# A tuned sum of reciprocals: new list for the last 48 rows, three large first loads, interleaved half rows

## Chip, cores, metric

The kernel runs on one core of one Trainium2 chip. The metric is the device time of one execution in microseconds (us), given as the median of several executions. Because this case turns on how executions of one and the same program differ, whole sets of executions are told beside the medians.

## The reference

```python
def setup_inputs():
    batch, seq, dim = 32, 512, 1024
    return {"x": np.abs(np.random.randn(batch, seq, dim)).astype(np.float32) + 1e-6}

def reference(x):
    return np.sum(1.0 / x, axis=-1).astype(np.float32)
```

There are 16,384 sums of 1024 reciprocals. On the chip they lie as 128 partitions by 128 rows. In what follows a "row" is one of these 128 columns of sums: a block of 128 x 1024 floats, 512 KB.

## The kernel before

The kernel takes the reciprocals of a pair of elements a and b from one logarithm and one exponential: 1/a + 1/b = (a + b) · exp(−ln(ab)). Each row is therefore split into two halves of 512, and several engines share the work. A static list gives the order of all operations; each letter is an operation, the number after it a row, `+n` means n rows in one instruction, `@b` a bank of PSUM or a slot of the product tile.

| letter | engine | what it does for a row |
|---|---|---|
| D | SP (load queue) | loads rows into a ring of 40 |
| P | POOL | product of the two halves, 128 x 512 |
| W | DVE | the same product, both halves read from SBUF |
| C, V | PE, DVE | PE copies the second half to PSUM; DVE multiplies the first half by that copy |
| L | ACT | logarithm of the product |
| E | ACT | exponential of minus the logarithm: in place, or to PSUM when it has a bank |
| S | PE | sum of the two halves in PSUM by two matmuls with the identity |
| R | DVE | final multiply and accumulate: 512 wide where the row has an S, else 1024 wide with the exponential broadcast |

The last two rows are handled as four half rows, numbered 126 to 129, so that less work stands behind the last load.

```python
    PLAN = """
        D9 D10 D14 D7 P0+2 C3@3 S2@0 V3 P2 L0+2@0 S3@1 E0+2@6 P4+2 S6@2 L2+2@2 R0 E2+2 R1
        # ... cut ...
        E122 R120 P124 S124@3 L123@8 R122 E123@7 W125 L124@15 S125@0 R123 P126 L125@16 E124
        P127 E125 R124 P128 S128@1 L126@17 R125 L127@0 P129 E126@7 S129@2 E127@6 R126 L128@1
        L129@9 R127 E128 E129 R128 R129
    """.split()
    # ... cut ...
    def place(r):                        # row -> row of the ring, offset, width of a half
        if r < LAST:                     # LAST = 126, F = 128, H = 512
            return r, 0, H
        q, part = divmod(r - LAST, 2)
        return LAST + q, part * H, H // 2
    # ... cut: note() keeps the dependences; its core is the loop that the change touches ...
        for other in needed:
            o_inst, o_engine, o_tick, _, _, o_known = other
            if o_tick <= known.get(o_engine, 0):
                tc.declare_no_dep(inst, o_inst, reason="implied by other waits")
                continue
            if o_engine == engine:
                continue
    # ... cut ...
            elif op in "WV":
                w = place(r)[2]
                in1 = xs(r, 1) if op == "W" else ps[:, copied[r], :w]
                inst = nc.vector.tensor_tensor(
                    out=prod[:, p, :w], in0=xs(r, 0), in1=in1, op=mult
                )
    # ... cut ...
            elif op == "R":
                # row: the exponential's slot (S rows) or the ring's row (the others)
                inst = nc.vector.tensor_tensor_reduce(
                    out=row, in0=row, in1=other, scale=S,
                    scalar=total if q in summed else 0.0,
                    op0=mult, op1=add, accum_out=total,
                )
```

## Time and profile before

| | before |
|---|---|
| time, median | 169.65 us (169.61 to 170.13) |
| span of the profiled run | 167.5 us |
| last load landed | 161.60 us |
| DVE done | 164.97 us |
| PE / DVE / ACT / POOL busy | 79 / 76 / 79 / 78% |
| W products / V products | 3 / 17 |

The prediction below reads the load queue, the landings and the tail. Three more lines of the same page matter later. PEclk is the granted clock of PE in 40 slices of the span, in tenths of full speed (9 is full); the next line is the group of W products (count, then busy us and mean ns of one); the last gives the shares of the chain of work that ended last.

```profile
PEclk9999999999699999999999999999999999999998
...
DMA 64%; DVE 11%; POOL 8%; PE 7%; ACT 5%; issue 2%; SPq 0%; DVEq 0%; POOLq 0%
...
L217 DVE TENSOR_TENSOR prod<-ring 128x512 f32<-128x512 f32 x3 | 2.0, 688 | 0.0
```

The reader is to see that the chain is 64% load time, and that one slice of PEclk, the 11th (42 to 46 us), reads 6. The timeline of PE shows what stands before it: a wait of 5.65 us for a load, in brackets.

```profile
43.64 2.08 PE L206 MATMUL ps<-ring,ident 128*128 128x512 f32 x2 [5.65 <-DMA ring<-in_x_dram]
```

I saw this 6 before predicting and made nothing of it.

### The profile page before, as it was taken

What the parts mean: (1) busy time and instruction counts of PE and PEld (TensorE: products, weight loads), DVE (VectorE), ACT (ScalarE), POOL (GpSimd) and SP (SyncE); (2) the same over time, 40 slices, a digit from 0 to 9 for tenths busy, and PEclk for the clock granted to TensorE, in tenths of its full rate; (3) what the DMA queues carried; (4) which work ended last, traced back from release to release, by engine and by line L of the source; (5) the groups of instructions that cost most, each with busy time, mean ns of one, the idle gap of its engine ahead of it and who ended that gap; (6) DMA issues with size and microseconds to landing.
All of it is one profiled execution on the core that took longest, in us unless ns stands there. A gap on an engine that the chain in (4) does not pass through costs nothing.

```text
span 167.5 us, 1308 instructions
## 1 busy us (share of the span) xinstructions
PE 132.1 (79%) x290; PEld 54.5 (33%) x290; DVE 127.5 (76%) x280; ACT 131.5 (79%) x155; POOL 131.0 (78%) x83
## 2 busy tenths in 40 slices
PE   0004996880599998999998999989979599977990
PEld 0002432330234343333433434334433144432450
DVE  0000585588049899979897898889999999999993
ACT  3000990994089999689989998999999999899991
POOL 1005946992599994998899998997989998999960
PEclk9999999999699999999999999999999999999998
DMA  6999999999899998998999999999999999999910
GB/s 202 440 431 434 401 470 438 438 438 438 383 438 430 483 446 385 434 460 351 470 431 421 438 417 425 432 420 440 407 429 426 410 425 421 417 407 411 393 63 16
DMA packets 4904, 67.25 MB, mean 402 GB/s; under 512 B 545, under 2 KB 673, under 8 KB 2209
## 3 DMA queue, kind: packets, MB, share of 16 engines
q1 hardware_dynamic: 4896, 67.18, 94.8%
q8 instruction: 2, 0.03, 0.1%
q14 instruction: 6, 0.04, 0.1%
HBM read 67.11 MB, written 0.07 MB: 401 GB/s over the span
## 4 chain that ended last, share of the span: by engine, by line
DMA 64%; DVE 11%; POOL 8%; PE 7%; ACT 5%; issue 2%; SPq 0%; DVEq 0%; POOLq 0%
DMA ring<-in_x_dram 64%; POOL prod L196 8%; DVE ring L264 7%; PE ps L229 4%; DVE prod L264 3%; PE ps L206 3%; ACT prod L239 3%; ACT ps L248 2%; ACT prod L248 1%; DVE prod L217 1%; SPq L184 0%; DVE sums L264 0%; DVEq L264 0%; POOLq L196 0%; DVEq L307 0%
## 5 line engine op out<-in xcount | busy, mean ns | idle before, releaser
L196 POOL TENSOR_TENSOR prod<-ring 128x1024 f32<-128x1024 f32 (+2 forms) x77 | 130.3, 1728 | 31.0 <-DMA ring<-in_x_dram 27.1
L229 PE MATMUL ps<-ring,ident 128*128 128x512 f32 (+1 forms) x256 | 116.3, 599 | 4.6 <-DVE sums L264 3.2
L239 ACT ACTIVATE prod<-prod 128x1024 f32<-128x1024 f32 (+3 forms) x77 | 67.8, 900 | 29.6 <-POOL prod L196 22.3
L264 DVE CUSTOM_DVE_ANT_1 ring<-ring,ps 128x1024 f32<-128x1024 f32 (+1 forms) x65 | 76.3, 1209 | 10.3 <-ACT ps L248 10.2
L229 PEld LDWEIGHTS ps<-ring,ident 128*128 128x128 f32 x256 | 48.3, 194 | 71.8 <-issue 51.1
L264 DVE CUSTOM_DVE_ANT_0 prod<-prod,ps 128x512 f32<-128x512 f32 (+1 forms) x63 | 40.6, 678 | 0.3
L206 PE MATMUL ps<-ring,ident 128*128 128x512 f32 x34 | 19.8, 672 | 26.6 <-DMA ring<-in_x_dram 26.5
L248 ACT ACTIVATE ps<-prod 128x1024 f32<-128x1024 f32 (+3 forms) x40 | 34.1, 859 | 1.4 <-DVE sums L264 0.7
L248 ACT ACTIVATE prod<-prod 128x1024 f32<-128x1024 f32 (+3 forms) x37 | 33.8, 924 | 0.7
L217 DVE TENSOR_TENSOR prod<-ring,ps 128x512 f32<-128x512 f32 x17 | 11.6, 684 | 26.5 <-PE ps L206 26.5
L206 PEld LDWEIGHTS ps<-ring,ident 128*128 128x128 f32 x34 | 6.2, 203 | 36.6 <-issue 18.3
L264 DVE DVE_READ_ACCUMULATOR2_ANT sums<- 128x1 f32 x130 | 10.7, 82 | 0.0
L217 DVE TENSOR_TENSOR prod<-ring 128x512 f32<-128x512 f32 x3 | 2.0, 688 | 0.0
L82 ACT ACT_TABLE_LOAD x1 | 1.3, 1283 | 0.7 <-PEq L296 0.7
L264 DVE CUSTOM_DVE_ANT_1 ring<-ring,ps,sums 128x512 f32<-128x512 f32 x1 | 0.7, 746 | 0.2 <-DVE sums L264 0.2
L264 DVE CUSTOM_DVE_ANT_0 prod<-prod,ps,sums 128x256 f32<-128x256 f32 x1 | 0.5, 479 | 0.2 <-DVE sums L264 0.2
masks.py:197 POOL MEMSET ident<- 128x128 f32 x1 | 0.2, 204 | 0.3 <-POOLq L296 0.3
masks.py:199 POOL TENSOR_SCALAR_AFFINE_SELECT ident<-ident 128x128 f32<-128x128 f32 x1 | 0.3, 293 | 0.1
L296 POOL MEMSET const-float32-0.0<- 128x1 f32 x1 | 0.1, 98 | 0.2 <-issue 0.2
L296 POOL MEMSET const-bfloat16-1.0<- 128x1 bf16 x1 | 0.1, 101 | 0.0
L296 POOL MEMSET const-uint8-127<- 128x1 uint8 x1 | 0.1, 101 | 0.0
L296 POOL MEMSET const-float32-1.0<- 128x1 f32 x1 | 0.1, 98 | 0.0
## 6 DMA issues: line engine op xcount, KB each, us to landing
ring<-in_x_dram SPq DMA_DIRECT2D x3, 3584.0 KB, 31.5
ring<-in_x_dram SPq DMA_DIRECT2D x2, 5120.0 KB, 26.2
ring<-in_x_dram SPq DMA_DIRECT2D x1, 7168.0 KB, 42.0
ring<-in_x_dram SPq DMA_DIRECT2D x1, 6144.0 KB, 33.4
ring<-in_x_dram SPq DMA_DIRECT2D x4, 1536.0 KB, 33.7
ring<-in_x_dram SPq DMA_DIRECT2D x6, 1024.0 KB, 28.9
ring<-in_x_dram SPq DMA_DIRECT2D x2, 2560.0 KB, 32.8
ring<-in_x_dram SPq DMA_DIRECT2D x1, 4608.0 KB, 13.8
```

Source lines behind the costliest of these rows:

```text
L82: nc.scalar.add_instruction(mybir.InstLoadActFuncSet(name=nc.get_next_instruction_name(), act_func_set_id=act_sets.index("natural_log_exp_ ...
L196: inst = nc.gpsimd.tensor_tensor(out=prod[:, p : p + m, :w], in0=ring[:, a : a + m, at : at + w], in1=ring[:, a : a + m, at + w : at + 2 * w],
L206: inst = nc.tensor.matmul(ps[:, b, : place(r)[2]], lhsT=ident, rhs=xs(r, 1), start=True, stop=True,)
L217: inst = nc.vector.tensor_tensor(out=prod[:, p, :w], in0=xs(r, 0), in1=in1, op=mult)
L229: inst = nc.tensor.matmul(ps[:, b, : place(r)[2]], lhsT=ident, rhs=xs(r, h), start=h == 0, stop=h == 1,)
L239: inst = nc.scalar.activation(out=pg, in_=pg, func=Ln, scale=S)
L248: inst = nc.scalar.activation(out=rc, in_=pg, func=Exp, scale=-1.0)
L264: inst = nc.vector.tensor_tensor_reduce(out=row, in0=row, in1=other, scale=S, scalar=total if q in summed else 0.0, op0=mult, op1=add, acc ...
L296: nc = _bacc.Bacc("TRN2", target_bir_lowering=False, num_devices=1)
```

## The change

Its intent is to shorten the tail and to balance the engines in the last 48 rows. There are three parts: a new list (three large first loads of 14, 12 and 14 rows instead of 9, 10, 14 and 7; single rows over the last 14; eight W products instead of three, mostly in rows 82 to 95); the four half rows in interleaved order (first half of row 126, first half of 127, second of 126, second of 127), so that a half never adds to the sum just before it; and bookkeeping that keeps dependences within one engine.

```diff
     PLAN = """
-        D9 D10 D14 D7 P0+2 C3@3 S2@0 V3 P2 L0+2@0 S3@1 E0+2@6 P4+2 S6@2 L2+2@2 R0 E2+2 R1
+        D14 D12 D14 P0+2 C3@3 S2@0 V3 P2 L0+2@0 C11@3 S3@1 E0+2@6 P4+2 V11 L2+2@2 R0 S6@2
 ... cut: the rest of the list; of the changed one, three lines from rows 81 to 99 and the end:
+        L81+2@18 P88+2 S86@2 R83 D1 D1 D1 E81+2 R82 S87@4 L88+2@0 W91 W86 D1 E88+2@6 W87 D1
+        D1 D1 W90 L85+2@20 S94@3 P94 R89 L87@17 E85+2 R88 P92 S95@5 L94@8 R86 E87 P93 R85
+        L90+3@2 R87 C97@7 P96 R81 E94 S98@0 V97 L93@9 P98 R94 L96@5 E93@7 S97@1 W95 E90+3@2
 ... cut ...
+        L119@7 S122@2 E121 R120 P123 L122@15 R121 E122 W124 L123@16 R122 L124@12 E123@7 W125
+        S125@0 E124@6 R123 P126 L125@13 P127 L126@14 S127@1 R124 E125 P128 L127@0 S128@2
+        E126@7 P129 R125 E127 S129@3 L128@1 R126 L129@20 E128 R127 E129 R128 R129
@@ place
-        q, part = divmod(r - LAST, 2)
+        part, q = divmod(r - LAST, F - LAST)
@@ note
+            if o_engine == engine:
+                continue
             if o_tick <= known.get(o_engine, 0):
                 tc.declare_no_dep(inst, o_inst, reason="implied by other waits")
-                continue
-            if o_engine == engine:
                 continue
```

## The prediction

> **What bounds the kernel now.** I read the page first (busy shares, slices, queues), then the waits of the load queue, then the landing time of every load, then the chain that ended last and the DVE timeline of the final microseconds. The page:

> ```profile
> span 167.5 us, 1308 instructions
> PE 132.1 (79%) x290; PEld 54.5 (33%) x290; DVE 127.5 (76%) x280; ACT 131.5 (79%) x155; POOL 131.0 (78%) x83
> ...
> DMA  6999999999899998998999999999999999999910
> ...
> q1 hardware_dynamic: 4896, 67.18, 94.8%
> ```

> Four compute engines are busy some 130 us each, the DMA engines 94.8% of the span, from the first slice to the next to last. So the loads are the floor of the body, and compute has some 30 us of idle to spend. What the queue itself waits for:

> ```profile
> SPq L184 <- DVE sums L264: 95.6, 14, 30.6
> SPq L184 <- DMA ring<-in_x_dram: 44.7, 17, 6.1
> ```

> These 140 us look alarming, but they are waits to *issue*: the load of row 112 was issued at 116.8 and landed at 143.8, so the transfers stay queued behind others. Reading the landings in order (middle one of each load's 16 counts) shows no hole: loads of 1, 2, 3, 7 and 14 rows land 1.28, 2.48, 3.69, 8.52 and 16.94 us after the one before. That is 1.205 us a row plus 0.07 us a load. The 16th count trails the middle one by 1.5 us from about 80 us on; it is the one that releases readers. The last load landed at 161.60, the load of row 125 at 159.01. The loads therefore fix about 161.6 of the 167.5 us. Behind stands a tail: DVE ends at 164.97, the output takes 2.5 us more, and the measured time is 2.1 us over the span (169.65 against 167.5). DVE in the tail:

> ```profile
> 159.04 0.69 DVE L217 TENSOR_TENSOR prod<-ring 128x512 f32<-128x512 f32 x1
> 159.65 1.21 DVE L264 CUSTOM_DVE_ANT_1 ring<-ring,ps 128x1024 f32<-128x1024 f32 x1
> ...
> 160.96 0.69 DVE L264 CUSTOM_DVE_ANT_0 prod<-prod,ps 128x512 f32<-128x512 f32 x1
> ...
> 161.71 0.69 DVE L264 CUSTOM_DVE_ANT_0 prod<-prod,ps 128x512 f32<-128x512 f32 x1
> ...
> 162.36 0.69 DVE L264 CUSTOM_DVE_ANT_1 ring<-ring,ps 128x512 f32<-128x512 f32 x1
> ...
> 163.21 0.75 DVE L264 CUSTOM_DVE_ANT_1 ring<-ring,ps,sums 128x512 f32<-128x512 f32 x1 [0.16 <-DVE sums L264]
> ...
> 163.89 0.41 DVE L264 CUSTOM_DVE_ANT_0 prod<-prod,ps 128x256 f32<-128x256 f32 x1
> ...
> 164.49 0.48 DVE L264 CUSTOM_DVE_ANT_0 prod<-prod,ps,sums 128x256 f32<-128x256 f32 x1 [0.18 <-DVE sums L264]
> ```

> The first is the product of row 125, at 159.04: it starts 0.03 us after its row landed, so the tail hangs on that landing. Then come the sums of rows 123, 124, 125 and of the four half rows. From start to start: a 512-wide step costs 0.61, a 1024-wide 1.14, a half row 0.61 or 0.34 by its form; adding to an earlier sum costs 0.07 more. The two half rows with "sums" among their inputs add to what the row just before them left; where an unheld step starts together with the accumulator read before it (163.89), these two start 0.24 and 0.26 us after it (162.97 and 164.23).

> [...] The kernel waits there, and the trace shows its price, the 0.24 and 0.26 us. [...] instructions with several waits may have EventSemaphore instructions put before them; the trace has them at 21 ns on DVE, with about 0.1 us from one to the held start when the queue has run dry. [...]

> **The change part by part.**

> *Loads.* 34 instead of 33, the same bytes: one more times 0.07. First loads 14, 12, 14 instead of 9, 10, 14, 7. The first rows land at 13.8 + 5 x 1.205 + 0.7 = 20.6 us instead of 14.56, so POOL, ACT and DVE start 6 us later. Is that paid at the end? Load queue: row 40 is needed in flight at 52 us and asks for rows 0 to 11 summed; at 1.03 us a row (DVE in the body: two 1.14 and two 0.61 per four rows plus 0.48 idle on ACT) from about 25 us they are done near 38. Margin 14 us; the same count for the later loads never leaves less than 6. No hole arises. POOL: a row pair takes 2.4, so 1.2 a row, less the one in eight that DVE multiplies, against 1.215 a row of landing. It is level with the landings at the next loads (rows 72 to 79 land at 102.0, P78 ends near 110.4), about where it is now. So the late start is absorbed: 0 us on the end.

> *Last 48 rows.* DVE work from row 80 on, by the list: now 22 rows of 0.61, 24 of 1.14, 10 products of 0.61, halves 1.9, 48.9 us; changed 23, 23, 12, halves 1.9, 49.4 us. Row 79 is summed near 113.8 with one product (0.6) done, leaving 48.8, hence an end of work at 162.6 if never stopped, against 163.3 by the same count now. Both are below the landing-driven end, with 2 us of small gaps to absorb. Single rows over the last 14: rows 114 and 116 land 1.28 us sooner, rows 117 on at the same time. 0 at the end.

> *Same-engine waits.* The edit in the bookkeeping keeps dependences within an engine. In the built order, DVE instructions that wait on DVE go from 2 to 21, POOL on POOL from 1 to 14. Nearly all ask for something long past. At up to 0.1 us each that is 2 us on DVE and 1.3 on POOL, mostly before 150 us where there is idle. In the tail I allow 0.1 to 0.3 us in all.

> *The tail.* The product of row 125 starts at its landing, 159.01 + 0.07 = 159.08, plus 0.03. Then the new order: product 0.61, row 123 1.14, row 124 1.14 (it was 0.61), row 125 0.61, then halves 0.61, 0.34 (was 0.68), 0.41, 0.48. Sum 5.34: 164.45 without gaps. Now the same sum is 0.61+1.14+0.61+0.61+0.61+0.68+0.34+0.48 = 5.08, ending at 164.12; measured 164.97, so gaps cost 0.85, of which 0.50 stand before the two accumulating halves and 0.31 before rows 124 and 125 on ACT and on the second wait. Interleaved, each half adds to the half two back, so most of the 0.50 goes; row 124 takes 1.14, so ACT runs ahead. Gaps left: 0.1 to 0.3. End 164.55 to 164.75, against 164.97.

> Do POOL and ACT allow it? The last half lands at 161.67; POOL's four halves pitch 0.69 and end near 162.7 as now (162.61). Counting ACT at its pitches (0.52 a 512-wide, 0.31 a half), the last exponential starts near 163.35 and ends at 163.75; its sum needs it at about 164.0. Yes, by 0.3 us.

> Sum: +0.07 for the load, +0.19 for the tail's work, -0.55 to -0.75 for its gaps: about -0.3 us. 169.65 - 0.35 = 169.3.

> **The rivals.**

> 1. *The late start is not absorbed.* Compute is then the bound and up to 6 us come at the end: 175. For it: the four engines are within 20% of the loads' rate. Against: 37 us of DVE idle, and POOL waits for loads nine times, 27.1 us in all. I give 2%.
> 2. *The kept same-engine waits cost what the interleaving saves.* The final half rows carry three waits each; at 0.1 us for each added wait the tail ends at 165.0: 169.65, no change. Likely enough, 25%.
> 3. *DVE, not the landing, sets the end.* DVE is idle only some 2 us from 112 us on. If the new order lines up worse with landings by 1 to 2 us, 170 to 171; if it lines up better, nothing, as landing rules. 10%.
> 4. *The slowest DMA engine.* The 1.5 us by which the 16th count trails arose between 52 and 80 us, where instruction fetches of 0.3 to 1.05 us stand in the trace. If they fall otherwise, the last landing moves by -0.7 to +0.7.

> **Range and chances.** Centre 169.3; rival 4 and the run spread (169.61 to 170.13) give +-0.5, rivals 2 and 3 lengthen the upper side: 168.7 to 170.0. Faster by 2% would need an end before the last landing's own chain (product, logarithm, exponential, sum: 2.3 us after 161.6, or 168.6 in time), so it is nearly excluded: 0.01. Slower by 2% needs rival 1: 0.02.

> **What would show it.** Changed profile: DMA share near 95% and no hole; first POOL product at 20.6; last landing at 161.5 to 161.8; product of row 125 within 0.1 us of its landing; the four half rows without a 0.2 us gap before accumulation; DVE end 164.5 to 164.8. I am wrong if DVE is behind when row 125 lands, if a load slice falls below 9 before the end, or if the last landing moves by over 0.3 us.

## The result

The changed kernel took 171.62 us in the median (executions of 171.20, 171.62 and 171.62; a fourth of 246.41 had a granted clock of 0.6 and is set aside). The kernel before, run beside it, took 169.69 us. The ratio is 1.010 with an interval of 1.007 to 1.013. Here and below a ratio is the mean time of one kernel's fast executions over that of the other's fast executions of the same rounds, so it is not quite the ratio of the medians. The class "within 2%" was right; the range, 168.7 to 170.0, missed by 1.6 us, and the sign was wrong. Three executions turned out to be too few: the interval does not hold the ratio that 22 later ones gave (below).

The page of the changed kernel, lines answering to those shown of before:

```profile
span 169.8 us, 1330 instructions
PE 132.2 (78%) x292; PEld 55.3 (33%) x292; DVE 129.9 (76%) x282; ACT 131.1 (77%) x153; POOL 129.8 (76%) x79
...
PEclk9999999999995699999999999999999999999997
DMA  6999999899999998999999999999999999999600
...
DVE 45%; PE 22%; DMA 12%; issue 11%; ACT 6%; another core or an unknown queue 3%; DVEq 0%
...
L217 DVE TENSOR_TENSOR prod<-ring 128x512 f32<-128x512 f32 x8 | 8.1, 1044 | 0.0
```

The loads did as predicted: no slice below 8 between the first and the last four (the page before has slices of 8 too, so the "below 9" among the prediction's signs of being wrong was set too high), the last landing at 161.71. But the chain that ended last is no longer the loads (64% before, 12% now); it is DVE and PE. Two other lines stand out: PEclk has two low slices (5 and 6), and the mean W product takes 1044 ns instead of 688. The tail confirms that DVE was late. The timeline of DVE:

```profile
161.74 0.68 DVE L217 TENSOR_TENSOR prod<-ring 128x512 f32<-128x512 f32 x1
162.40 1.22 DVE L264 CUSTOM_DVE_ANT_1 ring<-ring,ps 128x1024 f32<-128x1024 f32 x1
```

This is the product of row 125, predicted at 159.1. The row had landed at 159.15; DVE came to it 2.6 us later because it was still at earlier sums, which is the first of the prediction's own signs of being wrong. DVE finished at 167.25 instead of the predicted 164.55 to 164.75.

Where did the W products lose time? The timelines of DVE and of POOL around 122 and 130 us:

```profile
121.33 2.37 DVE L217 TENSOR_TENSOR prod<-ring 128x512 f32<-128x512 f32 x2
...
129.54 2.46 DVE L217 TENSOR_TENSOR prod<-ring 128x512 f32<-128x512 f32 x1
```

```profile
121.70 6.85 POOL L196 TENSOR_TENSOR prod<-ring 128x512 f32<-128x512 f32 x5 [2.14 <-ACT ps L248]
129.09 4.05 POOL L196 TENSOR_TENSOR prod<-ring 128x1024 f32<-128x1024 f32 x2 [0.54 <-DVE prod L217]
```

Taken one by one, the product of row 90 ran from 121.93 to 123.70 (1.77 us) and that of row 95 from 129.54 to 132.01 (2.46); the other six took 0.68 to 0.70. Each of the two began while a product of POOL was running (from 121.70, and a pair from 129.09) and ended about 0.55 us after POOL's had ended (123.15 and 131.46). The next product of POOL took 1.73 and 1.75 us instead of 1.28. Beyond 0.68 each, the two products took 1.09 + 1.78 = 2.9 us, about as much as DVE was late.

What happened at PEclk's low slices? PE stretch by stretch; the columns are the stretch, its length, PE's busy time (instructions), the granted clock, the DMA share and GB/s. I put the edges 3.41 us apart, where the clock changes.

```profile
44.58:48.00 3.42, 2.55 (x6) 1.00 1.20 520
48.00:51.41 3.41, 0.00 (x0) 1.00 0.93 401
51.41:54.83 3.42, 2.25 (x3) 0.50 0.97 417
54.83:58.24 3.41, 3.41 (x5) 0.50 0.96 418
58.24:61.65 3.41, 3.41 (x9) 1.00 0.97 418
```

PE idles from 47.5 to 52.6 us waiting for a load. After a stretch with no work the clock is exactly half, and it stays half for two stretches. The record of the clock in this trace has full clock for 27.31 us, half for 6.83 and full for 109.23, which is 8, 2 and 32 times 3.413 us; that of the kernel before has 23.89, 3.41 and 119.47 us, or 7, 1 and 35 times. Below, such a stretch of 3.413 us is called a window, and its ends are the edges.

### The profile page after: what moved, and what is told of

The parts are those of the page before. It is cut to its first block, busy times and chain, and to the rows that moved or that the text cites. A ratio compares the mean times of both kernels' runs of the same rounds, so it can differ in the third digit from the quotient of the medians.

```text
span 169.8 us, 1330 instructions
## 1 busy us (share of the span) xinstructions
PE 132.2 (78%) x292; PEld 55.3 (33%) x292; DVE 129.9 (76%) x282; ACT 131.1 (77%) x153; POOL 129.8 (76%) x79
## 3 DMA queue, kind: packets, MB, share of 16 engines
q1 hardware_dynamic: 5040, 67.18, 93.5%
## 4 chain that ended last, share of the span: by engine, by line
DVE 45%; PE 22%; DMA 12%; issue 11%; ACT 6%; another core or an unknown queue 3%; DVEq 0%
DVE ring L264 24%; PE ps L229 17%; DVE prod L264 13%; DMA ring<-in_x_dram 12%; DVE prod L217 7%; PE ps L206 5%; ACT ps L248 4%; DVE sums L264 2%; ACT prod L239 1%; ACT prod L248 1%; DVEq L264 0%; DVEq L307 0%
## 5 line engine op out<-in xcount | busy, mean ns | idle before, releaser
L229 PE MATMUL ps<-ring,ident 128*128 128x512 f32 (+1 forms) x264 | 119.1, 599 | 6.2 <-DVE sums L264 6.0
L239 ACT ACTIVATE prod<-prod 128x1024 f32<-128x1024 f32 (+3 forms) x76 | 68.0, 908 | 27.5 <-POOL prod L196 21.5
L264 DVE CUSTOM_DVE_ANT_1 ring<-ring,ps 128x1024 f32<-128x1024 f32 x64 | 75.0, 1207 | 4.2 <-ACT ps L248 4.2
L229 PEld LDWEIGHTS ps<-ring,ident 128*128 128x128 f32 x264 | 49.7, 193 | 74.7 <-issue 50.5
L264 DVE CUSTOM_DVE_ANT_0 prod<-prod,ps 128x512 f32<-128x512 f32 x64 | 41.3, 676 | 0.4 <-PE ps L229 0.4
L248 ACT ACTIVATE ps<-prod 128x1024 f32<-128x1024 f32 (+3 forms) x38 | 33.4, 883 | 6.3 <-DVE sums L264 4.6
L206 PE MATMUL ps<-ring,ident 128*128 128x512 f32 x28 | 16.8, 686 | 26.2 <-DMA ring<-in_x_dram 25.8
L248 ACT ACTIVATE prod<-prod 128x1024 f32<-128x1024 f32 (+3 forms) x38 | 34.8, 922 | 0.8
L217 DVE TENSOR_TENSOR prod<-ring,ps 128x512 f32<-128x512 f32 x14 | 9.6, 684 | 32.7 <-PE ps L206 32.7
L206 PEld LDWEIGHTS ps<-ring,ident 128*128 128x128 f32 x28 | 5.6, 217 | 34.2 <-issue 25.3
L264 DVE DVE_READ_ACCUMULATOR2_ANT sums<- 128x1 f32 x130 | 10.5, 81 | 0.0
L217 DVE TENSOR_TENSOR prod<-ring 128x512 f32<-128x512 f32 x8 | 8.1, 1044 | 0.0
L264 DVE CUSTOM_DVE_ANT_0 prod<-prod,ps,sums 128x256 f32<-128x256 f32 x2 | 1.0, 480 | 0.0
```

Source lines behind the costliest of these rows:

```text
L206: inst = nc.tensor.matmul(ps[:, b, : place(r)[2]], lhsT=ident, rhs=xs(r, 1), start=True, stop=True,)
L217: inst = nc.vector.tensor_tensor(out=prod[:, p, :w], in0=xs(r, 0), in1=in1, op=mult)
L229: inst = nc.tensor.matmul(ps[:, b, : place(r)[2]], lhsT=ident, rhs=xs(r, h), start=h == 0, stop=h == 1,)
L239: inst = nc.scalar.activation(out=pg, in_=pg, func=Ln, scale=S)
L248: inst = nc.scalar.activation(out=rc, in_=pg, func=Exp, scale=-1.0)
L264: inst = nc.vector.tensor_tensor_reduce(out=row, in0=row, in1=other, scale=S, scalar=total if q in summed else 0.0, op0=mult, op1=add, acc ...
```

## The experiments

Three theories stood at the start, and a fourth came out of the repeats. **Theory A**: the added W products meet POOL on DVE, and that alone is the loss. **Theory B**: the late start (three large loads) leaves the engines too late at the new list. **Kept waits** (theory C in the texts on record): the dependences kept within an engine cost time. **The clock** (theory D there, the fourth; D2 is the form in which place B makes the group at 170.8 to 171.3): PE at half speed makes the body or the tail late. In the later texts on record, "A" and "B" after the word place stand for two waits of PE for a load, not for theories: place A near 50 us and place B near 152 us. In each call the kernel before ran on the same chip, with medians of 169.70 to 169.81 and never outside 169.5 to 170.25.

### Products of rows 90 and 95 through PSUM

```diff
-  ... R82 S87@4 L88+2@0 ...  W90 ... S95@5 L94@8 ... W95
+  ... R82 S87@4 C90@5 L88+2@0 ...  V90 ... S95@5 C95@6 L94@8 ... V95
```

> The changed kernel; only the products of rows 90 and 95 differ: their second half goes through a PE copy to a PSUM bank, as 14 other rows of this kernel do, instead of DVE reading both halves from SBUF. In the changed kernel these two products took 1.77 and 2.46 us where six others took 0.68 to 0.70. Theory A (DVE with two SBUF inputs waits for the POOL product[...]): both products fall to 0.68, DVE gains 1.09 + 1.78 = 2.9 us, and the end moves from 167.25 to the landing-bound 164.5 to 164.8: about 169.1 to 169.5 us. Theory B (the larger first loads make all compute late): no change, 171.2 to 171.7. Theory C (the kept waits within an engine): no change.

The median was 170.25 and the ratio 1.0014 (0.9987 to 1.0041), which hides what matters. Of 20 executions, 8 took 168.82 to 169.16, 3 took 169.72 to 170.27, and 9 took 170.69 to 171.30. The six W products that were left took 0.68 each in the profile. So theory A holds for the mechanism but not for the whole loss: a slow group of executions is there without any product waiting. Its profiled execution (170.69) belonged to that group, and there PE's clock was halved at another place, from 152.9 to 156.3.

### The changed kernel once more

No edit.

> The changed kernel again, more times. Its runs with PE copies and with the old bookkeeping fell into two groups, 168.8 to 169.3 and 170.9 to 171.8; the first four runs of the change itself had only the second group. Theory D (PE's clock is halved for 3.4 us or more at one of two places[...], and the lateness that follows decides): two groups here too, near 169 and 171.3. Theory A alone (the two products of 1.77 and 2.46 us are always there): one group, 171.2 to 171.7.

Of 22 executions, 12 took 168.79 to 169.15, 7 took 170.82 to 171.23 and 3 took 171.68 to 171.97. The median is 169.12 and the ratio 1.0001 (0.9973 to 1.0028). The same program thus has two groups, some 2 us apart; the kernel before has one. The record labels the three highest "slow" and leaves them out of the ratio (likewise 7 of 20 and 2 of 12 in two runs below). That label only says that an execution lies over 1.5% above the fastest of its call; the first result's 171.62 did not get it, because nothing faster stood beside it. Its granted clock of 0.973 is no other state of the chip either: half clock in the two windows shown above (6.8 us) and after the last matmuls (2.4 us) adds up to it. The seven at 170.82 to 171.23 count as fast, so the two groups do not rest on the label. The three executions of the first result had all been in the upper group. The profiled one fell in the lower (169.08), so the two profiles of the same program can be laid side by side:

```profile
span 167.3 us, 1330 instructions
...
PEclk9999999999998799999999999999999999999998
```

```profile
46.59:50.00 3.41, 1.91 (x4) 1.00 1.13 488
50.00:53.42 3.42, 1.27 (x3) 1.00 0.98 419
53.42:56.83 3.41, 3.41 (x5) 0.50 0.93 404
56.83:60.24 3.41, 3.41 (x9) 1.00 1.03 447
```

PE waited at the same place, but the window edges lay 2.0 us later (50.00 against 48.00). The wait was cut in two, one part of 44% of a window (PE busy 1.91 of 3.41), which left the clock full, and one of 63%, which halved it; the next window was busy throughout, so one window at half clock was enough, not two. DVE and POOL then met otherwise:

```profile
120.53 1.28 DVE L217 TENSOR_TENSOR prod<-ring 128x512 f32<-128x512 f32 x2
...
127.72 0.73 DVE L217 TENSOR_TENSOR prod<-ring 128x512 f32<-128x512 f32 x1
```

```profile
121.60 6.30 POOL L196 TENSOR_TENSOR prod<-ring 128x512 f32<-128x512 f32 x5 [2.15 <-ACT ps L248]
```

The same two products (1.28 instead of 2.37) were done 0.2 us after POOL began instead of starting 0.23 us after it. And the tail came out as predicted:

```profile
159.26 0.69 DVE L217 TENSOR_TENSOR prod<-ring 128x512 f32<-128x512 f32 x1
159.87 1.22 DVE L264 CUSTOM_DVE_ANT_1 ring<-ring,ps 128x1024 f32<-128x1024 f32 x1
...
163.37 0.42 DVE L264 CUSTOM_DVE_ANT_0 prod<-prod,ps 128x256 f32<-128x256 f32 x1
...
163.71 0.48 DVE L264 CUSTOM_DVE_ANT_0 prod<-prod,ps,sums 128x256 f32<-128x256 f32 x1
...
164.23 0.48 DVE L264 CUSTOM_DVE_ANT_0 prod<-prod,ps,sums 128x256 f32<-128x256 f32 x1
```

The product of row 125 starts 0.02 us after its landing (159.24); a single gap of 0.12 us is left before the last half row; DVE ends at 164.71.

### The kernel before with seven of its V products as W

```diff
-  ... C83@5 ... V83 ... V89 ... V92 ... V95 ... V104 ... V106 ... V117
+  ...           W83 ... W89 ... W92 ... W95 ... W104 ... W106 ... W117
```

> The kernel before; the products of rows 83, 89, 92, 95, 104, 106 and 117 on DVE read both halves from SBUF, and their seven PE copies are gone. Everything else as before. Theory A: each such product that starts while POOL multiplies waits for the rest of that POOL product (0 to 1.28 us, by chance of phase some 0.6 on average), DVE has only about 1 us to spare from 112 us on, so 1 to 4 us slower: 170.5 to 173.5. Theories B and C: same or slightly faster (PE has 3 us less work), 169.4 to 169.8.

The four executions took 170.83 to 171.21, median 171.0, ratio 1.0067 (1.0047 to 1.0087). Four of the seven products (rows 95 to 117 of the list) took 1.15, 0.92, 1.25 and 1.51 us, and that of row 125 took 0.87, so DVE lost 2.3 us to POOL, and the kernel was 1.2 us slower. W products in the last third of a kernel can cost this much in the old list as well. The number is not a clean price: in its profile PE also had half the clock from 124.2 to 131.0.

### The first loads alone

```diff
-        D14 D12 D14 P0+2 ...
+        D9 D10 D14 D7 P0+2 ...
```

> The changed kernel with the first 40 rows loaded as 9, 10, 14, 7 as before, instead of 14, 12, 14. Theory B: compute starts 6 us sooner, DVE reaches row 79 some 1 to 1.75 us sooner (the changed kernel summed row 79 at 115.5, I had predicted 113.8), so 170.0 to 170.6. Theory A alone: the late start is absorbed before row 80 and the two waits for POOL stay, 171.2 to 171.7.

Early first loads with the new list took 177.93 us (177.46 to 179.96), ratio 1.050, the reverse of what theory B said. The clock line of its profile (of the slowest of the four):

```profile
PEclk9999855996599999999999999999996999999996
```

The list starts its engines in the order and at the pace of late loads. With early ones PE runs dry three times (19.0 to 26.9, 38.7 to 43.7, 60.0 to 61.8 us) and its clock is halved from 21.0 to 31.3 and from 41.5 to 48.3. Row 79 was summed at 119.79 instead of 114.7 to 115.5, five W products met POOL (1.75 to 2.84 us each), and DVE ended at 175.16. The run does not test whether a late start is free; it shows that load sizes and list are one part, not two, and it suggests that lateness around row 80 turns into more lateness.

### The bookkeeping of before

```diff
@@ note
-            if o_engine == engine:
-                continue
             if o_tick <= known.get(o_engine, 0):
                 tc.declare_no_dep(inst, o_inst, reason="implied by other waits")
                 continue
+            if o_engine == engine:
+                continue
```

> The changed kernel with the bookkeeping of before, which drops dependences within one engine when another wait implies them. Theory C: the 19 more waits of DVE on DVE and 13 of POOL on POOL cost 0.5 to 2 us: 169.6 to 171.1. Theories A and B: within 0.2 us of the changed kernel, 171.2 to 171.7.

Of 20 executions, 8 took 168.84 to 169.25, 5 took 170.95 to 171.24 and 7 took 171.43 to 171.82; ratio 1.0001. The lower group is that of the changed kernel (168.79 to 169.15), so the kept waits cost nothing that can be measured in the whole time, and the upper group is there without them.

### Idle matmuls before the waits of PE

If the clock makes the upper group, giving PE something to do in its two waits must remove it. The added operation multiplies the identity by itself into a bank that the next real matmul overwrites:

```diff
+            elif op == "H":
+                for _ in range(r):
+                    inst = nc.tensor.matmul(
+                        ps[:, b, :P], lhsT=ident, rhs=ident, start=True, stop=True
+                    )
+                    note("PE", inst, [], [("bank", b)])
```

**Place A alone** (`P26 H22@3 C27@3`, 22 matmuls ahead of the wait near 50 us):

> The changed kernel with 22 idle 128x128 matmuls of the identity put before the copy of row 27, to fill the 5 us in which PE waits for the load of rows 26 to 39 (47.5 to 52.6); they write a bank that is free then. Theory D: no halved clock at 51 to 58 us in any run, row 40 summed near 73.7 instead of 76.4; the runs near 171 that start with it go, those with a halved clock at 153 stay: a mixture of 169 and 171. Theory A: if the two long products come from the order of the list and not from this lateness, all runs stay near 171.5.

Five executions took 168.88 to 169.12, ratio 0.9956, and no slice of the profile had half the clock. I took this for proof, and it was not. The same kernel again:

> The kernel with the 22 idle matmuls before the copy of row 27 again: its five runs were all at 168.9 to 169.1, though its PE still waits from 150.5 to 152.8. Theory D2: about half the runs are at 170.8 to 171.3 this time, and the first five were luck (0.55 to the fifth, 5%). If the first place makes both groups: all at 168.8 to 169.2 again.

Of 12 executions, 5 took 168.88 to 169.39 and 7 took 170.86 to 172.31. The first five had been luck. The profile (171.06) shows place B. PE stretch by stretch, first this kernel, then the lower-group execution of the changed kernel:

```profile
150.70:154.10 3.40, 1.19 (x3) 1.00 1.03 412
154.10:157.50 3.40, 3.40 (x5) 0.50 1.02 402
```

```profile
149.00:152.40 3.40, 1.67 (x4) 1.00 1.03 412
152.40:155.80 3.40, 2.83 (x7) 1.00 1.02 408
```

In the new list rows 117 to 119 have no work for PE, and S120 waits for a row that lands at 152.7, so PE idles from about 150.7 to 153.0. That is 2.3 us, two thirds of a window. When a window edge falls as in the first fence, one window is 65% idle (3.40 − 1.19 of 3.40), and five matmul records fill the next, where a window at full clock holds nine (the last line of the first result's windows above). When the edge falls inside the wait, as in the second, the parts are 51% and 17%, and the clock stays full.

**Place B alone** (`P120 H8@3 S120@0`):

> The changed kernel with the 8 idle matmuls before the first sum of row 120 alone (PE waits there from 150.7 to 153.0); the wait for rows 26 to 39 is left as it is. In ten profiles every 3.41 us window[...] that PE idled for 0.59 of or more was followed by half clock, none of 0.56 or less. The wait at 150.7 can fill 0.67 of a window, so by the phase of the window about half the runs are hit. Theory D2 (this place makes the group at 170.8 to 171.3): that group goes; what stays is some 1 in 6 runs at 171.4 to 172 from two halved windows at 51 to 58 us. If the first place makes both groups: 4 in 10 runs stay at 170.8 to 172.

Six executions took 168.80 to 169.40, ratio 0.996 (0.9948 to 0.9972). PE's timeline shows the filling: 16 records, since each of the 8 stands in the trace as two records, and a wait of 0.50 us left instead of 2.29.

```profile
150.83 1.95 PE L216 MATMUL ps<-ident 128*128 128x128 f32 x16
153.28 4.96 PE L235 MATMUL ps<-ring,ident 128*128 128x512 f32 x11 [0.50 <-DMA ring<-in_x_dram]
```

**Both places** (22 at A, 8 at B), and both with the PSUM copies of rows 90 and 95:

> As the run before, with 8 more such matmuls before the first sum of row 120, where PE waits from 150.9 to 153 for a load and two profiles had the clock halved from 153 to 156.4. Theory D: both sources gone, one group at 168.8 to 169.3. Theory A alone: 171.2 to 171.7.

> Both: products of rows 90 and 95 by a PE copy, and the idle matmuls at the two places. Theory A with D: nothing is left that delays DVE, so the landing sets the end, one group at 168.6 to 169.2. If neither counts: 171.2 to 171.7.

Both places: 22 executions of 168.60 to 170.44, median 169.12, ratio 0.9974 (0.9961 to 0.9986). With the copies: 14 of 168.83 to 170.31, median 169.12, ratio 0.9977. No execution of the 36 lies at 170.5 or above, where the changed kernel had 10 of 22. Once the clock stays full the copies add nothing. Eight of the 36 lie between 169.64 and 170.44, which the clock does not explain. One of them was profiled (170.31), and it suggests another cause: the last count of the output's store came at 167.53, 1.3 us after the middle one (166.21), beside a fetch of 16 KB of instructions from 164.88 that took 1.47 us. In the profiled execution at 168.60 such a fetch came at 161.77, ahead of the store, and the last count trailed the middle one by 0.1 us. That is at most half of the scatter: four of the eight have a longer span, 167.6 being the most among executions below 169.5, and theirs 168.3 to 168.7; in the other four 2.1 to 2.7 us lie outside the span, where the changed kernel has 1.7 to 1.9, and none of those was profiled.

**Both places with fewer, wider matmuls** (6 and 4 of 512 columns), to have fewer instructions to fetch:

> The changed kernel with 6 and 4 idle matmuls of 512 columns at the two places, in place of 22 and 8 of 128 columns. With 30 small ones some runs took 169.5 to 170.4, and one such profile shows a third 16 KB instruction fetch beside the output's store, which landed 1.3 us late on one DMA engine. With 20 fewer matmuls that fetch should not be needed: one group at 168.7 to 169.2, none over 169.5. If the late store has another cause, the scatter to 170.4 stays.

Thirteen executions of 169.61 to 170.10, median 169.71, ratio 0.9997. The scatter is gone, but the expected 168.7 to 169.2 was missed: each wide matmul stands in the trace as two records 0.43 us apart, so the four at B held PE from 150.40 to 153.83, 1.1 us past the landing of row 120 (152.71), and DVE ended at 165.35. In the lower-group execution of the changed kernel PE takes up that row 0.14 us after its landing. This is a dose by accident, and not a clean one, as the matmuls at A changed too: with PE 1.0 us later at place B the kernel was 0.6 to 0.7 us slower (169.71 against 169.12 and 169.03).

### The interleaving alone, and undone

The kernel before with the new `place`:

> The kernel before with the four half rows in interleaved order and nothing else. From its tail: the waits of 0.24 and 0.26 us before the two accumulating half rows go, two rows of 0.07 for the added input stay, so DVE ends 0.3 to 0.5 us sooner: 169.2 to 169.4. If the waits were covered by the exponential anyway: 169.7.

This run is no evidence: it gave a wrong result (relative error 0.18) and took 205.9 us. Interleaved, half row 127 lies in the ring's place of row 87, and the old list loads it ahead of the sum of row 87. With that load moved behind `R87` it is right:

```diff
-        S89@5 R84 D1 D1 D1 D1 L87@21 E90@7 ... R87 D1 D1
+        S89@5 R84 D1 D1 D1 L87@21 E90@7 ... R87 D1 D1 D1
@@ place
-        q, part = divmod(r - LAST, 2)
+        part, q = divmod(r - LAST, F - LAST)
```

> The kernel before with the half rows in interleaved order alone. My first try put the load of a half row ahead of the sum that frees its place and gave a wrong result; here the load stands after it. The waits of 0.24 and 0.26 us before the accumulating half rows go: 0.3 to 0.5 us faster than before, 169.2 to 169.4. If they were covered anyway: 169.7.

Nine executions of 169.03 to 169.47, median 169.34, ratio 0.9977 (0.9967 to 0.9987): 0.39 us gained, DVE ends at 164.69. The opposite test takes the changed kernel, fills place B and puts the half rows back in sequence:

> The changed kernel with the 8 idle matmuls before row 120 and the half rows one after the other, as before. If the interleaved order gives the gain: 0.3 to 0.5 us above the 169.0 of the same kernel with interleaved halves, 169.3 to 169.5. If the new list of the last rows gives it: 169.0.

Of 12 executions, 5 took 169.25 to 169.53 (median 169.29, or 0.38 above the 168.91 of the changed kernel's lower group) and 7 took 171.90 to 172.10; those seven count as slow state and are not in the ratio of 0.9975. So the interleaving is worth 0.4 us both ways. The run shows something else as well: with B filled and A open, an upper group is still there, near 172. In its profile (171.90) the clock was halved for two windows from 51.8 to 58.6, the sum of row 40 came at 76.52 and the products of rows 90 and 95 took 1.77 and 2.18 us. That is the profile of the first result again, so by this one profile place A alone makes this group.

### Making PE late at place A on purpose

If lateness at A and the meeting with POOL are cause and effect, wide idle matmuls at A (B filled throughout) must bring the loss back at full clock, and the copies of rows 90 and 95 must take it away. The edits are `P26 G7@3 C27@3` and `P26 G10@3 C27@3`, where G is a matmul of 512 columns. With 7:

> The changed kernel with the 8 idle matmuls before row 120, and 7 idle matmuls of 512 columns (14 passes of 0.43, 6.0 us) before the copy of row 27. They keep the clock full but hold PE some 2.4 us beyond the landing of rows 26 to 39, about what two halved windows did (row 40 summed at 76.4 instead of 73.9). Theory A after D: the products of rows 90 and 95 wait for POOL, over 1 us each, and the end is 1.5 to 2.5 us late: 170.6 to 171.6, in every run. If the lateness is absorbed before row 80, as in the kernel before: 168.9 to 169.4.

> The same, with the products of rows 90 and 95 through a PE copy. Theory A after D: the lateness is absorbed and nothing waits for POOL: 168.9 to 169.6, at least 1 us below the run before this one. If the lateness itself reaches the end: as the run before.

Four executions each: 168.89 to 169.34 (ratio 0.9961) without and 168.86 to 169.23 (0.9956) with the copies. The dose was too small: the matmuls started at 47.3, earlier than I had counted, and the sum of row 40 came at 74.35, only some 0.5 us late. All eight executions were in the lower group. With 10:

> As the earlier run with 7 wide idle matmuls before the copy of row 27, but with 10: 20 passes of 0.43 from 47.3, so PE takes up row 27 near 55.9 instead of 53.3. Row 26 then near 60.8 (58.2 there, 60.4 in the first profile of the change), row 40 near 76.5. Theory A after D: the products of rows 90 and 95 take over 1.2 us each and the end is late in every run: 170.8 to 171.8. If the lateness alone decided nothing and the clock did: 168.9 to 169.4.

> The same lateness with the products of rows 90 and 95 through a PE copy. Theory A after D: absorbed, 168.9 to 169.6, over 1 us below the run before this one. If lateness itself reaches the end: as the run before this one.

The timeline of PE shows the dose, 20 records for 10 matmuls, and the first real matmul at 55.98 instead of 52.15 and 52.59:

```profile
47.40 8.75 PE L218 MATMUL ps<-ident 128*128 128x512 f32 x20
55.98 1.02 PE L206 MATMUL ps<-ring,ident 128*128 128x512 f32 x2
```

Without the copies it took 174.93 us (ratio 1.031) and W products met POOL: row 82 took 2.85, rows 86, 87 and 90 took 1.75 to 1.76 each. The loss came back, but larger than the expected 170.8 to 171.8, and row 95's product, at 0.68, was not part of it. With the copies it took 174.60 (1.028): rows 82, 86 and 87 met POOL for 2.00, 1.76 and 1.75. My expectation for the second, 168.9 to 169.6, failed: with more lateness the other W products of that stretch meet POOL instead. Nor are the two profiles equally late: row 79 was summed at 116.05 without and 117.10 with the copies, which act only after it. PE's lateness with the clock full up to these products (in both it is halved only later, for one window near 130) does bring a loss, but copies of two rows do not protect the list.

## Why the prediction was wrong, and where it was right

**What failed is the step "Both are below the landing-driven end, with 2 us of small gaps to absorb" of the part on the last 48 rows.** It put row 79 near 113.8, counted 48.8 us of DVE work behind it with every product at 0.61, and so had DVE's work end at 162.6, before the landings let the tail end. In the first result row 79 was summed at 115.54 and two products took 2.9 us more than counted: 115.54 + 48.8 + 2.9 = 167.2, and DVE ended at 167.25, busy for all 47.00 of the 47 us from 112 to 159. DVE's work, and not the landing of row 125, set the end. In the lower group the same sum gives 114.71 + 48.8 + 0.1 = 163.6, still below the landing-driven end, and there the end came as predicted. So two terms were mis-sized, row 79 by 0.9 to 1.7 us and the products by up to 2.9. Behind what parts the first result from the lower group stood an unspoken assumption: that PE's matmuls last what they lasted before. The 6 in PEclk of the page before said otherwise. The rest of row 79's lateness is not the clock at A: with A filled it came at 114.06 to 114.69. Why stays open.

**The step to the range failed with it.** It read: "Centre 169.3; rival 4 and the run spread (169.61 to 170.13) give +-0.5". The spread of the kernel before was carried over to a kernel whose spread was another one. The centre is 0.4 above the lower group (median 168.91); the upper group, 170.8 to 172.0, is what the first executions hit. That was bad luck: the median of the 22 later executions, 169.12, lies inside the range, but a prediction of one time for a program with two would have been no better for it.

**Slips in the sums.** None of them moves the result. The DVE work by the list comes to 48.8 (not 48.9) and 49.5 (not 49.4) us; the tail's work grows by 5.34 - 5.08 = 0.26, not 0.19; two 1.14, two 0.61 and 0.48 per four rows are 1.00 us a row, not 1.03; and in the profile before DVE was idle for 1.0 us from 112 us to its end, not "some 2".

**The phase acts once more, before place A, where PEclk does not show it.** With the new loads PE begins near 20.7 us with matmuls 0.85 us apart; they come 0.43 apart from the edge on at which the trace records its first full clock, 23.6 to 26.8 us by the execution. (The page's slices read 9 there all the same: the trace has no record of the clock before that edge.) The later this edge, the later row 25 is summed, and the shorter the wait at A (PE goes on at 52.0 to 52.6 in all six profiles):

| profile with A open | first full clock | row 25 summed | wait at A | windows halved at A |
|---|---|---|---|---|
| change, first result | 24.12 | 52.97 | 5.10 | two |
| sequential halves, B filled | 24.48 | 53.20 | 4.77 | two |
| B filled | 24.78 | 53.37 | 4.61 | one |
| change, lower group | 26.11 | 53.99 | 3.65 | one |
| PSUM copies of rows 90, 95 | 26.60 | 54.15 | 3.56 | none |
| bookkeeping of before | 26.80 | 54.27 | 3.26 | none |

The last two are the ones whose clock was halved at B. So in these six profiles one phase goes with everything that follows, and a later start of the full clock does not mean a later end.

**How the lateness reached the end.** These are times from the traces, in us; the excess is what the W products took beyond 0.68 each.

| execution | clock halved at | row 79 summed | excess of W products | row 91 summed | DVE end |
|---|---|---|---|---|---|
| change, lower group | A, one window | 114.71 | 0.1 | 132.27 | 164.71 |
| 7 wide matmuls at A, B filled | nowhere | 115.20 | 0.1 | 132.74 | 164.96 |
| change, first result | A, two windows | 115.54 | 2.9 | 135.42 | 167.25 |
| sequential halves, B filled | A, two windows | 115.67 | 2.6 | 135.26 | 167.53 |
| 10 wide matmuls at A, B filled | 129.9 to 133.3 | 116.05 | 5.4 | 138.47 | 170.49 |
| the same with copies | 128.6 to 132.0 | 117.10 | 3.5 | 138.44 | 170.46 |
| early first loads | 21 to 31, 41 to 48 and 134 to 137 | 119.79 | 6.6 | 143.37 | 175.16 |
| PSUM copies of rows 90, 95 | B | 115.06 | 0.0 | 132.70 | 166.30 |
| bookkeeping of before | B | 114.12 | 0.9 | 132.09 | 166.57 |

Two windows of half clock at A instead of one make row 79 0.8 us late (115.54 against 114.71). That is little, but row 90's product then starts 0.23 us after POOL's instead of ahead of it, and two products lose 2.8 us. From row 91 on, in all rows of the table without a halved clock at B, 31.8 to 32.4 us follow: DVE has next to no idle time there to absorb anything. With the clock halved at B it is 33.6 to 34.5, with and without products that met POOL (in the last row of the table, those of rows 91 and 125 took 1.12 us each).

**Point by point.**

- Loads: right. The last landing came at 161.71 and 161.80 (predicted 161.5 to 161.8), no hole. The first product of POOL started at 20.66 (20.6).
- Late start absorbed: right in the lower group only. Row 79 was predicted near 113.8 and came at 114.7; the margin was there, but it ended 0.8 us further on.
- "10 products of 0.61 ... changed ... 12": wrong as a constant. In these profiles a W product took 0.61 from start to start unless POOL was at a product that still had over about 0.15 us to run (in the first result one that began with 0.15 us left took 0.70 us, one with 0.06 left 0.68). Over all 20 profiles 41 were lengthened, to as much as 2.85 us, and each ended 0.55 us after the product of POOL that it met. Of the V products, with one input in PSUM, 235 began while POOL had over 0.2 us left of a product, and none took over 0.69.
- Same-engine waits: the allowance of 0.1 to 0.3 us was too high. In the lower groups the span is 0.1 us longer with the kept waits (167.15 against 167.04 in the mean), and the whole time is the same.
- The tail: right. End 164.55 to 164.75 predicted, 164.71 measured in the lower group; the interleaving alone is worth 0.39 us, taken from the gaps as told.
- The rivals: 3 came closest ("DVE, not the landing, sets the end", 170 to 171, 10%), in number and in its form, not in its cause. I had no rival in which the same program has two times.

Of the lower group's gain over the kernel before, 0.8 us in the median (168.91 against 169.70), 0.26 are in DVE's end (164.71 against 164.97). The rest lies mostly outside the span: time minus span is 2.0 to 2.3 us for the kernels with the old list and 1.7 to 1.9 for most with the new one. The new list with the bookkeeping of before has 1.95 in the mean, against 1.79 with the new bookkeeping, so some 0.16 of it goes with the bookkeeping. What it is stays open.

**Also open:** whether lateness at place A would be absorbed if no W product could meet POOL. The run meant to show it (10 wide matmuls with copies) still had three that met. That no execution of the kernel with copies of rows 90 and 95 lay above 171.3, where 3 of 22 and 7 of 20 did without, fits the story but doesn't prove it.

**A version that beats both.** The changed kernel with idle matmuls at both places took 0.9974 of the time before over 22 executions; with 7 wide ones at A and 8 narrow ones at B, 0.9961 over 4. It gains nothing over the change's good executions (169.12 against 168.91 in the median), but removes its bad ones.

## What to carry to other kernels

Read the line of the granted PE clock, and list PE's waits of 2 us or more before trusting a spread: here waits of 2.3 us and of 3.3 to 5.1 us halved the clock in some executions and not in others, so run a kernel often enough to see two groups, and do not take five equal times for proof. Where DVE is near its limit and POOL reads SBUF, look at when the DVE products with two SBUF inputs start: here such a product took 0.68 us by itself and 1.77 when it began 0.23 us after one of POOL's; with one input in PSUM, begun while POOL had over 0.2 us left of a product, none took over 0.69. This static list has its loads' pace built in (with early first loads it took 177.93 us), so change the two together.
